# Scatters between zero columns in the Pool queue, and the fallback branch ahead of the last batch's scatters

## Chip, core, metric

The kernel runs on one core of a Trainium2 chip. The metric is the device time of one execution in microseconds (us), as a median over several executions. Ratios are the mean time of one kernel's fast runs over the mean of the other's fast runs of the same rounds, on the same chip, so they are not quite the ratio of the medians that stand beside them.

## The reference

```python
B, S, H = (8, 2048, 2560)          # scores (B, S, S), values (B, S, H), float32
best_j = np.argmax(scores, axis=2)
gathered = values[b_idx, best_j, :].copy()
out = np.zeros_like(values)
np.add.at(out, (b_idx, best_j, slice(None)), gathered)
```

Output row j of a batch is values row best_j of the position that chose it, summed over all positions whose argmax is j. Since the row added is always row j itself, the output row is `values[j]` times the number of times that j was chosen. So every row is of one of three kinds: never chosen (a zero row), chosen once (a plain copy), chosen more often (copy times a count).

## The kernel before

VectorE finds the argmax of each row of scores, TensorE counts with one-hot matrices, and the counts become three lists of row numbers for each batch. Pool then issues indirect DMAs of 128 rows each. Row numbers that are out of range are skipped, so a DMA may carry fewer than 128 rows.

- *copies* (`copy_once`): values to out inside the HBM, 16 a batch, for rows that were chosen once;
- *zero columns* (`zeros`): from a row of zeros in the SBUF, 7 a batch, 12 in the last one;
- *gather and scatter*: 5 each a batch. A gather brings 128 many-counted rows into one of six slots of `vbig`, ScalarE multiplies them by their counts, a scatter writes them out.

```python
        def gathers():
            for k in range(MCAP):                       # MCAP = 5
                v = stage()                             # next of 6 slots
                gather(v, mi[:, k:k + 1])
                nc.scalar.activation(out=v, in_=v, ..., scale=mc[:, k:k + 1])
                staged.append(v)
                if rest:
                    copy_once(rest.pop(0))

        def zeros():
            for k in range(ZLAST if b == B - 1 else ZCAP):     # 12 or 7
                scatter(zrow[:], zi[:, k:k + 1], free_running)
                if rest:
                    copy_once(rest.pop(0))
        ...
            gathers()
            zeros()
        for k in range(MCAP):
            scatter(staged[k], mi[:, k:k + 1])
        ...                                             # after all batches:
    nc.gpsimd.wait_ge(landed, 16 * n_free[0])
    more = nc.values_load(over_i[0:1, 0:1], engines=[mybir.EngineType.Pool], ...)
    with tc.If(more > 0):                               # lists longer than 7, 5 or 12 columns
        ...                                             # scatter and gather the rest
```

Copies and zero columns are `free_running`: they count on one semaphore, `landed`, that only the end waits for. Gathers and scatters have the framework's own semaphores ("tracked"). A gather must wait until the scatter that last read its slot has landed. In the last batch, `level_engines` (cut here) spreads the zero rows unevenly over 16 groups of partitions, so that all DMA engines get the same number of rows in total. The fallback in the `If` isn't taken for this draw. When a branch isn't taken, the framework's code for that path waits for all tracked DMAs issued before it, and then adds to their semaphores what the branch would have added; that is the `INC_SWDGE_SEM` of the profiles.

Of the kernel before, what the change touches and what calls it, by code (L numbers as in the profile page):

```python
# [36 lines left out]
def kernel(  # L37
# [6 lines left out]
    nc = tc.nc  # L44
    B, S, S2 = scores.shape
    _, _, H = values.shape
    assert S == S2
    NT = S // P
# [6 lines left out]
    NM = NT // 2  # L55
    NE = 16
    LE = P // NE
    ZCAP, MCAP = 7, 5
    ZLAST = 12
    CORR = 56  # L60

    values_flat = values.rearrange("b s h -> (b s) h")
# [56 lines left out]
    zrow = ctx.enter_context(nc.sbuf_tensor([P, H], FP32))  # L119
# [6 lines left out]
    zero_i = ctx.enter_context(nc.sbuf_tensor([P, B * NT], INT32))  # L126
    many_i = lists.tile([P, B * NM], INT32)
# [7 lines left out]
    landed = tc.alloc_semaphore("landed")  # L135
    n_free = [0]
# [8 lines left out]
    def gather(v, idx):  # L145
        nc.gpsimd.indirect_dma_start(  # L146
            out=v, out_offset=None, in_=values_flat[:, :],
            in_offset=bass.IndirectOffsetOnAxis(ap=idx, axis=0), bounds_check=B * S - 1, oob_is_err=False)

    def scatter(v, idx, note=writes_out):  # L150
        note(nc.gpsimd.indirect_dma_start(  # L151
            out=out_flat[:, :], out_offset=bass.IndirectOffsetOnAxis(ap=idx, axis=0),
            in_=v, in_offset=None, bounds_check=B * S - 1, oob_is_err=False))

    vslot = [0]

    def stage():
        v = vbig[:, vslot[0] * H:(vslot[0] + 1) * H]
        vslot[0] = (vslot[0] + 1) % NV
        return v  # L160
# [46 lines left out]
    def level_engines(rank):  # L207
# [27 lines left out]
        fits = lev.tile([P, 1], FP32)  # L235
        nc.vector.tensor_single_scalar(out=fits[:], in_=zeros, scalar=float(NE * (NT * LE - CORR)), op=ALU.is_le)
        nc.vector.tensor_scalar(out=more[:], in0=more[:], scalar1=float(CORR), scalar2=fits[:, 0:1], op0=ALU.min, op1=ALU.mult)
        all_more = lev.tile([P, 1], FP32)
# [29 lines left out]
    def value_steps(b, cnt_ps):  # L268
# [12 lines left out]
        def copy_once(t):  # L281
            free_running(scatter_rows_in_dram(
                nc, out_flat[:, :], values[b, t * P:(t + 1) * P, :], one_i[:, t:t + 1], last_row))
# [68 lines left out]
        rest = list(range(first, NT))  # L352
        staged = []

        def gathers():
            for k in range(MCAP):
                v = stage()
                gather(v, mi[:, k:k + 1])
                nc.scalar.activation(out=v, in_=v, func=mybir.ActivationFunctionType.Copy, bias=0.0,  # L359
                                     scale=mc[:, k:k + 1])  # L360
                staged.append(v)
                if rest:
                    copy_once(rest.pop(0))

        def zeros():
            for k in range(ZLAST if b == B - 1 else ZCAP):
                scatter(zrow[:], zi[:, k:k + 1], free_running)
                if rest:
                    copy_once(rest.pop(0))


        if b == 0:
            zeros()

            for _ in range(10):
                yield
            gathers()
        else:
            gathers()
            zeros()  # L380
        for k in range(MCAP):
            scatter(staged[k], mi[:, k:k + 1])
        yield

    ET = mybir.EngineType
    with tc.manual_schedule(engines={ET.PE, ET.DVE, ET.Activation, ET.SP}):
        pending = iter(())
        for b in range(B):
            cnt_ps = psum_c.tile([P, NT], FP32)
            for _ in count_steps(b, cnt_ps):  # L390
                next(pending, None)
            for _ in pending:
                pass
            pending = value_steps(b, cnt_ps)
            if b < 2:
                for _ in range(4):
                    next(pending)
        for _ in pending:
            pass
        full = fin.tile([1, 2], FP32)  # L400
        nc.vector.tensor_reduce(out=full[:, 0:1], in_=tots[0:1, 0, 0:B - 1], op=ALU.max, axis=mybir.AxisListType.X)
        nc.vector.tensor_reduce(out=full[:, 1:2], in_=tots[0:1, 1, :], op=ALU.max, axis=mybir.AxisListType.X)
        over = fin.tile([1, 3], FP32)
        nc.vector.tensor_single_scalar(out=over[:, 0:1], in_=full[:, 0:1], scalar=float(ZCAP * P), op=ALU.is_gt)
        nc.vector.tensor_single_scalar(out=over[:, 1:2], in_=full[:, 1:2], scalar=float(MCAP * P), op=ALU.is_gt)
        nc.vector.tensor_single_scalar(out=over[:, 2:3], in_=most[0:1, :], scalar=float(ZLAST * LE), op=ALU.is_gt)
        over_i = fin.tile([1, 1], INT32)
        nc.vector.tensor_reduce(out=over_i[:], in_=over[:], op=ALU.max, axis=mybir.AxisListType.X)

    nc.gpsimd.wait_ge(landed, 16 * n_free[0])  # L410
    more = nc.values_load(over_i[0:1, 0:1], engines=[mybir.EngineType.Pool], min_val=0, max_val=2)
    with tc.If(more > 0):
        for b in range(B):
            for k in range(ZLAST if b == B - 1 else ZCAP, NT):
                scatter(zrow[:], zero_i[:, b * NT + k:b * NT + k + 1])
            for k in range(MCAP, NM):
                v = stage()
                i = b * NM + k
                gather(v, many_i[:, i:i + 1])
                nc.gpsimd.tensor_scalar(out=v, in0=v, scalar1=many_c[:, i:i + 1], scalar2=None, op0=ALU.mult)  # L420
                scatter(v, many_i[:, i:i + 1])


# [28 lines left out]
```

## Time and profile before

| | before |
|---|---|
| time, median of 6 runs | 840.62 us (839.85 to 841.81) |
| profiled span | 838.4 us |
| last row landed (the trace's semaphore updates) | 829.95 us |
| from there to the end of the span, "tail" | 8.4 us |
| VectorE's last instruction ends | 697.2 us |

What bounds the kernel is read in the prediction below. Four stretches more of the kernel before will be needed later (us from and to, length; busy time of PE and PEld, which are TensorE, DVE, which is VectorE, ACT, which is ScalarE, and POOL; granted clock; mean busy share of the 16 DMA engines; GB/s):

```profile
635.00:640.00 5.00, 0.00 (x0) 0.00 (x0) 4.97 (x4) 0.00 (x0) 3.35 (x5) 1.00 0.99 389
695.00:700.00 5.00, 0.59 (x16) 0.48 (x15) 1.42 (x12) 0.00 (x0) 1.51 (x2) 1.00 0.93 385
790.00:795.00 5.00, 0.00 (x0) 0.00 (x0) 0.00 (x0) 3.76 (x2) 3.78 (x5) 1.00 1.01 424
795.00:800.00 5.00, 0.00 (x0) 0.00 (x0) 0.00 (x0) 2.43 (x1) 3.83 (x4) 1.00 1.01 424
```

The DMA moves about 424 GB/s where all 16 engines have work. At 635 and 695 us it is lower; I read this as some engines having nothing queued.

### The profile page before, as it was taken

To read this page: it belongs to the slowest core of one execution; us is meant where nothing else is said; L and a number is where in the kernel's file an instruction comes from. 1 tells how busy PE (TensorE), PEld (TensorE's weight loads), DVE (VectorE), ACT (ScalarE), POOL (GpSimd) and SP (SyncE) were. 2 spreads that over 40 slices of the span, in tenths; PEclk is the share of its full clock that TensorE was granted. 3 is DMA by queue.
4 is the path that set the end of the run, shared out by engine and by line. 5 is a ranking of instruction groups with operands and counts; after the bars stand their busy time and mean duration, and the time that the engine had idled before them with its cause. 6 is when DMAs were issued, how large, how long until landed. Compare 5 with 4: busy or idle time off the path is not lost.

```text
span 838.4 us, 2053 instructions
## 1 busy us (share of the span) xinstructions
PE 14.7 (2%) x273; PEld 14.1 (2%) x273; DVE 678.6 (81%) x794; ACT 102.9 (12%) x43; POOL 274.3 (33%) x277
## 2 busy tenths in 40 slices
PE   0000000000000000000000000000000000000000
PEld 0000000000000000000000000000000000000000
DVE  7999999999999999999999999999999992000000
ACT  2000001401300002200003200013100500500500
POOL 0000743267101254130263300551305724734720
DMA  9999999999999999999999999999999999999992
GB/s 383 426 429 431 380 421 422 421 407 428 422 431 426 425 427 431 426 426 427 427 428 428 428 427 425 429 425 427 427 426 409 420 425 412 417 416 418 418 418 117
DMA packets 48111, 347.04 MB, mean 414 GB/s; under 512 B 19014, under 2 KB 19014, under 8 KB 19014
## 3 DMA queue, kind: packets, MB, share of 16 engines
q0 software_dynamic: 38736, 212.67, 61.4%
q1 hardware_dynamic: 9360, 134.22, 37.6%
q14 instruction: 13, 0.11, 0.0%
q8 instruction: 2, 0.03, 0.0%
HBM read 354.42 MB, written 300.15 MB: 781 GB/s over the span
## 4 chain that ended last, share of the span: by engine, by line
DVE 69%; DMA 12%; POOL 5%; issue 4%; another core or an unknown queue 4%; ACT 0%; PE 0%; POOLq 0%
DVE am L185 32%; DVE mx L184 29%; DMA out_dram<-vbig,many_i 9%; DMA vbig<-in_values_dram,many_i 3%; POOL out_dram L151 2%; DVE oh_lo L194 2%; POOL out_dram L33 2%; DVE oh L321 2%; POOL vbig L146 1%; DVE lo L190 1%; DMA vbig<-in_scores_dram 1%; DVE oh_hi L198 0%; ACT vbig L359 0%; DVE put L336 0%
## 5 line engine op out<-in xcount | busy, mean ns | idle before, releaser
L185 DVE FIND_INDEX8 am<-mx,s_tile 128x8 uint32<-128x2048 f32 x116 | 265.0, 2285 | 0.0
L184 DVE MAX8 mx<-s_tile 128x8 f32<-128x2048 f32 x116 | 264.3, 2278 | 0.0
L33 POOL DMA_INDIRECT out_dram<-in_values_dram,ones_i x128 | 131.2, 1025 | 157.1 <-DVE m L292 119.0
L359 ACT ACTIVATE vbig<-vbig,many_c 128x2560 f32<-128x2560 f32 x40 | 96.7, 2426 | 693.8 <-DMA vbig<-in_values_dram,many_i 693.8
L146 POOL DMA_INDIRECT vbig<-in_values_dram,many_i x40 | 42.4, 1060 | 230.2 <-DMA out_dram<-vbig,many_i 182.3
L151 POOL DMA_INDIRECT out_dram<-vbig,many_i x40 | 38.9, 972 | 122.5 <-ACT vbig L359 118.0
L151 POOL DMA_INDIRECT out_dram<-zrow,zero_i x61 | 60.6, 994 | 18.9 <-issue 18.9
L184 DVE MAX8 mx<-vbig 128x8 f32<-128x2048 f32 x12 | 27.4, 2279 | 4.8 <-DMA vbig<-in_scores_dram 4.8
L185 DVE FIND_INDEX8 am<-mx,vbig 128x8 uint32<-128x2048 f32 x12 | 27.4, 2285 | 0.0
L194 DVE TENSOR_TENSOR oh_lo<-lo,lane_f 128x512 bf16<-128x512 uint32 x32 | 22.2, 693 | 0.4
L321 DVE TENSOR_TENSOR oh<-lo,fill_f 128x2048 f16<-128x2048 uint32 x8 | 18.3, 2291 | 0.3
L203 PE MATMUL cnt_ps<-oh_hi,oh_lo 128*128 128x16 bf16 x128 | 8.1, 174 | 578.3 <-DVE oh_hi L198 578.3
L203 PEld LDWEIGHTS <-oh_lo 128*128 128x128 bf16 x128 | 8.4, 105 | 578.1 <-DVE oh_lo L194 577.1
L185 DVE MATCH_VALUE_LOAD am<-mx,s_tile 128x8 f32 x116 | 10.7, 92 | 4.0
L198 DVE TENSOR_TENSOR oh_hi<-hi,lane_f 128x64 bf16<-128x64 uint32 x32 | 6.9, 217 | 0.0
L190 DVE TENSOR_SCALAR lo<-am 128x4 uint32<-128x4 uint32 x32 | 5.8, 183 | 1.1
L339 PE MATMUL l_ps<-put,oh 128*128 128x32 f16 x128 | 4.7, 188 | 68.5 <-DVE put L336 68.5
L339 PEld LDWEIGHTS <-oh 128*128 128x128 f16 x128 | 4.6, 104 | 69.6 <-DVE oh L321 59.2
L192 DVE TENSOR_SCALAR hi<-am 128x4 uint32<-128x4 uint32 x32 | 5.5, 172 | 0.0
L326 DVE TENSOR_TENSOR ez<-hi,lane_f 128x256 f16<-128x256 uint32 x8 | 3.3, 418 | 0.0
L336 DVE TENSOR_TENSOR put<-ez,row_f 128x256 f16<-128x256 f16 x8 | 3.3, 417 | 0.0
L347 DVE TENSOR_SCALAR e<-l_ps 128x32 f32<-128x32 f32 x8 | 1.5, 185 | 2.0 <-PE l_ps L339 2.0
(91 smaller groups left out, 60.3 us busy)
## 6 DMA issues: line engine op xcount, KB each, us to landing
s_tile<-in_scores_dram SPq DMA_DIRECT2D x58, 2048.0 KB, 12.0
vbig<-in_scores_dram SPq DMA_DIRECT2D x5, 2048.0 KB, 32.6
vbig<-in_scores_dram SPq DMA_DIRECT2D x2, 1024.0 KB, 6.1
out_dram<-in_values_dram,ones_i POOLq DMA_INDIRECT x128, 28.3
out_dram<-zrow,zero_i POOLq DMA_INDIRECT x61, 25.4
vbig<-in_values_dram,many_i POOLq DMA_INDIRECT x40, 32.3
out_dram<-vbig,many_i POOLq DMA_INDIRECT x40, 46.4
```

The source lines that it names most:

```text
L33: return eng.add_instruction(ins)
L146: nc.gpsimd.indirect_dma_start(out=v, out_offset=None, in_=values_flat[:, :], in_offset=bass.IndirectOffsetOnAxis(ap=idx, axis=0), bounds_ ...
L151: note(nc.gpsimd.indirect_dma_start(out=out_flat[:, :], out_offset=bass.IndirectOffsetOnAxis(ap=idx, axis=0), in_=v, in_offset=None, bound ...
L184: nc.vector.max(out=mx[:], in_=rows)
L185: nc.vector.max_index(out=am[:, g, :], in_max=mx[:], in_values=rows)
L190: nc.vector.tensor_single_scalar(out=lo[:], in_=am[:, :, 0], scalar=P - 1, op=ALU.bitwise_and)
L194: nc.vector.tensor_tensor(out=oh_lo[:], in0=lo[:].unsqueeze(2).to_broadcast([P, G, P]), in1=lane_f[:].unsqueeze(1).to_broadcast([P, G, P]) ...
L198: nc.vector.tensor_tensor(out=oh_hi[:], in0=hi[:].unsqueeze(2).to_broadcast([P, G, NT]), in1=lane_f[:, 0:NT].unsqueeze(1).to_broadcast([P, ...
L203: nc.tensor.matmul(out=cnt_ps[:], lhsT=oh_lo[:, g, :], rhs=oh_hi[:, g, :], start=(t == 0), stop=(t == NT - 1))
L321: nc.vector.tensor_tensor(out=oh[:], in0=lo[:].unsqueeze(2).to_broadcast([P, NT, P]), in1=fill_f[:].unsqueeze(1).to_broadcast([P, NT, P]), ...
L339: nc.tensor.matmul(out=l_ps[:], lhsT=oh[:, t, :], rhs=put[:, t, :], start=(t == 0), stop=(t == NT - 1))
L359: nc.scalar.activation(out=v, in_=v, func=mybir.ActivationFunctionType.Copy, bias=0.0, scale=mc[:, k:k + 1])
```

## The change

Its intent: scatters go ahead of the last three zero columns of a batch, so that slots come free sooner and Pool has work queued behind them. In the last batch the branch goes ahead of the scatters and of 8 zero columns, so that its cost lies under moving data and not at the end. The fallback uses one slot instead of cycling through six. (Cut: the declarations of `ZHEAD`, `last_staged` and `nz`, which is 12 in the last batch and 7 in the others, batch 0, where all zero columns stay ahead of the gathers, and the fallback's body, where only `v = stage()` moves out of the loops.)

```diff
-        def zeros():
-            for k in range(ZLAST if b == B - 1 else ZCAP):
+        def zeros(columns):
+            for k in columns:
...
         else:
             gathers()
-            zeros()
+            zeros(range(ZHEAD))                    # ZHEAD = 4
+        if b == B - 1:
+            while rest:
+                copy_once(rest.pop(0))
+            last_staged.extend(staged)
+            return
         for k in range(MCAP):
             scatter(staged[k], mi[:, k:k + 1])
+        if b > 0:
+            zeros(range(ZHEAD, nz))
...
-    nc.gpsimd.wait_ge(landed, 16 * n_free[0])
     more = nc.values_load(over_i[0:1, 0:1], engines=[mybir.EngineType.Pool], min_val=0, max_val=2)
     with tc.If(more > 0):
...
+    b = B - 1
+    for k in range(MCAP):
+        scatter(last_staged[k], many_i[:, b * NM + k:b * NM + k + 1])
+    for k in range(ZHEAD, ZLAST):
+        scatter(zrow[:], zero_i[:, b * NT + k:b * NT + k + 1], free_running)
+    nc.gpsimd.wait_ge(landed, 16 * n_free[0])
```

More of the change, by code (lines that the diff above doesn't have):

```diff
@@ L59 @@
     ZLAST = 12
+    ZHEAD = 4
     CORR = 56
@@ L155 @@
     vslot = [0]
+    last_staged = []
     def stage():
@@ L369, in zeros @@
                     copy_once(rest.pop(0))
+        nz = ZLAST if b == B - 1 else ZCAP
         if b == 0:
-            zeros()
+            zeros(range(nz))
             for _ in range(10):
@@ L379, in value_steps @@
             gathers()
-            zeros()
+            zeros(range(ZHEAD))
[4 more added lines that the diff above has]
+            return
         for k in range(MCAP):
             scatter(staged[k], mi[:, k:k + 1])
+        if b > 0:
+            zeros(range(ZHEAD, nz))
+        assert not rest
         yield
@@ L408 @@
         nc.vector.tensor_reduce(out=over_i[:], in_=over[:], op=ALU.max, axis=mybir.AxisListType.X)
-    nc.gpsimd.wait_ge(landed, 16 * n_free[0])
     more = nc.values_load(over_i[0:1, 0:1], engines=[mybir.EngineType.Pool], min_val=0, max_val=2)
     with tc.If(more > 0):
+        v = stage()
         for b in range(B):
@@ L416 @@
             for k in range(MCAP, NM):
-                v = stage()
                 i = b * NM + k
```

## The prediction

> **What bounds the kernel now.** I read the page first (parts 1, 2, 3), then the table of stretches, the waits of Pool, the time line of Pool at the end, and last the lines of the end of the program one by one.
>
> ```profile
> PE 14.7 (2%) x273; PEld 14.1 (2%) x273; DVE 678.6 (81%) x794; ACT 102.9 (12%) x43; POOL 274.3 (33%) x277
> ```
>
> The first line is a trap: VectorE is 81% busy, but the time line ends its last reduction at 697.2 us, and the span is 838.4. What is busy to the end is the DMA.
>
> ```profile
> DMA  9999999999999999999999999999999999999992
> q0 software_dynamic: 38736, 212.67, 61.4%
> q1 hardware_dynamic: 9360, 134.22, 37.6%
> ```
>
> Queue q1 (the scores) and q0 (all that Pool issues) together fill 99% of 16 engines' span. 212.67 MB of rows is exactly 20,762 rows of 10,240 bytes: 16,384 rows of the output, plus 4,378 rows that are counted twice or more and are moved twice (gather, then scatter). I counted those from the reference's own draw. The change moves no byte fewer. The stretches of the end (us; then busy time of PE, PEld, DVE, ACT, POOL; clock; DMA share; GB/s):
>
> ```profile
> 740.00:760.00 20.00, 0.00 (x0) 0.00 (x0) 0.00 (x0) 0.00 (x0) 2.04 (x2) 1.00 1.02 419
> 780.00:800.00 20.00, 0.00 (x0) 0.00 (x0) 0.00 (x0) 12.14 (x5) 15.18 (x16) 1.00 1.02 425
> 820.00:825.00 5.00, 0.00 (x0) 0.00 (x0) 0.00 (x0) 0.00 (x0) 0.00 (x0) 1.00 0.54 227
> 825.00:830.00 5.00, 0.00 (x0) 0.00 (x0) 0.00 (x0) 0.00 (x0) 0.00 (x0) 1.00 0.17 72
> 830.00:835.00 5.00, 0.00 (x0) 0.00 (x0) 0.00 (x0) 0.00 (x0) 0.00 (x0) 1.00 0.00 0
> ```
>
> Pool does nearly nothing from 740 to 760 and still the DMA share is 1.02. So Pool's long waits,
>
> ```profile
> POOL vbig L146 <- DMA out_dram<-vbig,many_i: 182.3, 19, 41.5
> POOL out_dram L151 <- ACT vbig L359: 118.0, 25, 9.9
> ```
>
> (gathers that wait for a slot of vbig, scatters that wait for the multiplication) lie over a full queue and cost almost nothing. Two things are left at the end: a fall of the DMA share from 820 to 830, where some of the 16 engines are done and others are not, and 8.4 us after the last landing (830.0) in which nothing moves. That tail is made of these:
>
> ```profile
> L410 POOLq EVENT_SEMAPHORE  x1: 17/17/17, 817.2 to 817.2; - x1
> L411 POOLq TENSOR_LOAD <-over_i x1: 626/626/626, 817.3 to 817.3; - x1
> L412 POOLq COMPARE_BRANCH  x1: 53/53/53, 818.2 to 818.2; - x1
> L412 POOLq EVENT_SEMAPHORE  x5: 17/43/43, 822.2 to 830.0; - x5
> L412 POOLq INC_SWDGE_SEM  x1: 1340/1340/1340, 830.1 to 830.1; - x1
> L447 POOLq DRAIN  x3: 40/107/6121, 831.4 to 838.1; - x3
> ```
>
> At 817.2 the rows that carry no tile semaphore have landed; the register load and the branch follow; the path where the branch is not taken begins at 822.2 and waits on the semaphores of gathers and scatters until 830.0; one instruction that adds to those semaphores takes 1.34 us; a Pool drain takes 6.12 us; barriers take 0.8 us.
>
> **What the Trainium skill says.** "DMA: Bandwidth & Descriptors", Issuing engines are not separate DMA queues: DMAs of all issuers run on the same 16 engines and interleave. The trace agrees (share 1.02 with q0 alone, 1.01 with both), so a new order in Pool's queue creates no bandwidth. The same page, Why a DMA increments its semaphore by 16 and not by 1: each engine posts its own +1, and only the full 16 means landed. The trace agrees and shows how much that matters here: the 16 updates of the last gather stand from 777.6 to 795.1 us, so the engines run up to 17.5 us apart. "Runtime: NRT & Kernel Launch", Instruction fetch mechanics: a taken branch out of the fetched window stalls for a fetch. The trace agrees: 3.9 us from the end of the branch (818.3) to the next instruction (822.2). No page states what a Pool drain behind software DMAs costs.
>
> **The change part by part.** *(a) Batches 1 to 6: five scatters go ahead of zero columns 4 to 6 and the three copies between them.* Same instructions. They land earlier by what now stands behind them: about 258 zero rows (770 less 4 x 128) and 3 x 45 copied rows, 393 rows or 25 to an engine. An engine moves 418/16 = 26.1 GB/s, a row in 0.39 us: 10 us. So Pool's wait for slots should shrink by some 8 to 10 us a batch, but that wait is covered by the DMA. What it can recover is the time in which leading engines ran dry. In 5-us stretches from 620 to 815 the rate fell visibly below 425 at 630 to 640 (407, 382), 695 to 705 (394, 404) and a few more; all deficits there sum to about 3.4 us of the mean engine, and a part of that is skipped rows, not idleness. I put down 0 to 3 us.
>
> *(b) Last batch: the branch ahead of the scatters.* The register load (0.63), the arithmetic (0.19) and the branch with its fetch (4.0) were already hidden in the fall from 817 to 830; they gain nothing. The add to the semaphores (1.34) leaves the tail. The drain (6.12) stands at the end of the program in both kernels. If it is a walk over everything Pool has issued, it stays; if it is work left over by the add, it goes. The price: the untaken path waits, as now, for every tracked DMA issued before it, and the last of them is now the fifth gather of the last batch. It landed at 795.1 on the slowest engine. Until then Pool issues none of the 5 scatters and 8 zero columns behind it.
>
> Does the DMA run dry meanwhile? I replayed the levelling code on the draw. All engines get 1,298 or 1,299 rows (one 1,293), but the zeros of the last batch per engine are between 20 and 76: the engines that had many copied rows lag, the others lead and get more zeros. Behind the fifth gather stand 8 copies and zero columns 0 to 3. *Slowest engine*: 24 + 20 = 44 rows, 17 us, busy until 812: the scatters come long before. *Leading engine* (76 zeros): 777.6 us, then 21 copied rows and 32 zeros, 53 x 0.39 = 21 us: dry at 798. The first scatter can start at 795.1 + 0.1 + 1.34 + 1.0 (one indirect DMA on Pool, 0.97 in its row of part 5) + about 1 of start = 798.5. So it is just caught. Behind it: 34 scattered rows and 44 zeros, 78 x 0.39 = 30 us, then about 1 us to land: 829.5. Before, it was 777.6 + 131 rows = 828 to 830. *The last landing hardly moves.* Pool's 13 issues at 1.28 us end at about 814 and are not the limit.
>
> *(c) Fallback branch with a single slot*: not taken for this draw (7 x 128 = 896 against at most 780 zeros; 5 x 128 = 640 against 565; 12 x 8 = 96 against 76). No time.
>
> Sum: last landing 829.5 (was 830.0), no add, drain 6.1 and barriers 0.9: span 836.5. The median stands 2.3 us above the profiled span, so about 838.7; with (a)'s gain at the slowest engine, up to 2 us less.
>
> **The rivals.** *The drain is a leftover of the add.* It starts 0.03 us after the add ends, and by then Pool had issued nothing for 28 us, which speaks for it; that the drain at the program's start took 0.2 us with no DMA behind it speaks for the other reading. If the leftover also blocks nothing behind it, the tail falls to about 1 us: 832.5. If it blocks Pool's next issue instead, the first scatter comes at 804.5, the leading engines idle 6 us, the landing goes to 835.5 and the tail to 1 us: 838.5, again no gain. I give the drain 70% to stay.
>
> *The slots free earlier and the engines close up.* The mean engine was done at about 822.4 (the 16 updates of the last scatter stand from 815.7 to 830.0), so perfect levelling would gain 7 us more, with the drain kept 831, without it 825. Against it: the chain above ties the leading engines to the slowest engine's fifth gather, which is not moved by freeing slots, since all work ahead of it in the ring is the same.
>
> *The branch becomes a real wait.* Under a full DMA the fetch of the untaken path may take longer than 4 us, and the leading engines may be further ahead, as (a) lets them run: each us by which the first scatter comes later than they run dry is a us on the end. With 4 to 6 us lost: 843.
>
> **Range and chances.** 70% for the drain kept (836 to 840), about 20% for the drain gone (829 to 834), the rest for a lengthened landing. Weighted I say 837.0, range 830.0 to 843.0. Faster by over 2% means below 824.1: it would need the drain gone and the engines levelled at once, 5%. Slower by over 2% means above 857.4, 17 us lost: 3%.
>
> **What would show it.** In the profile after: bytes and packets of q0 unchanged; the DMA share 1.0 until about 820; Pool's wait for slots clearly below 182 us, with the total hardly moved; the first scatter of the last batch issued 2 to 3 us after the fifth gather's full landing near 795; the last landing at 829.5 +/- 3; a drain of about 6 us at the end and no add ahead of it. It is wrong if the drain is under 1 us (then I mis-assigned it), if the first scatter comes 8 us after the gather (the add blocks), or if the fall of the DMA share at the end becomes much shorter than 15 us (then levelling, which I discounted, was the gain).

## The result

The changed kernel takes 839.79 us (median of 6 runs, 838.97 to 840.14) against 840.62; the ratio is 0.9989 with an interval of 0.9976 to 1.0002. That can't be told from no change. The profiled span is 837.9 us. It is inside the range, but the forecast of 837.0 was a gain of 3.6 us, and 0.8 came.

The same stretches of the changed kernel, with those of the end:

```profile
635.00:640.00 5.00, 0.00 (x0) 0.00 (x0) 4.93 (x6) 0.00 (x0) 3.78 (x5) 1.00 1.02 422
695.00:700.00 5.00, 0.59 (x16) 0.58 (x16) 3.73 (x16) 0.00 (x0) 4.32 (x3) 1.00 1.02 422
790.00:795.00 5.00, 0.00 (x0) 0.00 (x0) 0.00 (x0) 3.66 (x3) 0.00 (x0) 1.00 0.96 400
795.00:800.00 5.00, 0.00 (x0) 0.00 (x0) 0.00 (x0) 1.29 (x1) 2.81 (x3) 1.00 0.84 350
...
820.00:825.00 5.00, 0.00 (x0) 0.00 (x0) 0.00 (x0) 0.00 (x0) 0.00 (x0) 1.00 0.47 172
825.00:830.00 5.00, 0.00 (x0) 0.00 (x0) 0.00 (x0) 0.00 (x0) 0.00 (x0) 1.00 0.09 37
```

The low stretches at 635 and 695 us are filled. A new and deeper one stands between 790 and 800, where there was none before. Pool's waits (us in total, times, longest):

```profile
POOL out_dram L152 <- ACT vbig L361: 237.4, 35, 25.3
...
POOL vbig L147 <- DMA out_dram<-vbig,many_i: 80.5, 16, 18.1
```

The wait for slots fell from 182.3 to 80.5 us, and the wait for the multiplication rose from 118.0 to 237.4. Most of both lies over a full DMA queue. The last one does not. It shows in Pool's time line:

```profile
776.98 0.98 POOL L33 DMA_INDIRECT out_dram<-in_values_dram,ones_i  x1 [0.30 <-issue]
796.58 0.97 POOL L152 DMA_INDIRECT out_dram<-vbig,many_i  x1 [18.62 <-ACT vbig L361]
```

Pool issues nothing for 18.6 us. The view puts that down to the multiplication; the instructions of the branch, and the last line of the end of the program, say what it was:

```profile
L422 POOLq EVENT_SEMAPHORE  x5: 17/43/14687, 772.7 to 793.9; - x5
L422 POOLq COMPARE_BRANCH  x1: 53/53/53, 767.6 to 767.6; - x1
L422 POOLq INC_SWDGE_SEM  x1: 1381/1381/1381, 794.0 to 794.0; - x1
...
L464 POOLq DRAIN  x3: 40/107/7675, 829.4 to 837.6; - x3
```

The path that isn't taken waits 14.7 us, until the fifth gather has landed on the slowest DMA engine at 793.8, and adds to the semaphores for 1.38 us; 2.8 us after that landing the first scatter goes out. The last row lands at 829.20 us, 0.75 earlier than before, which is less than this moment varies from profile to profile (see below). The add is gone from the tail. But the Pool drain at the end takes 7.68 us instead of 6.12, so the tail is 8.7 us and not the 7.0 that I had summed.

Two questions are left. Why did the filled stretches bring only 0.75 us? And why did the drain grow?

### The profile page after: what moved, and what is told of

Its sections match the earlier page's. It is cut to its first block, busy times and chain, and to the rows that moved or that the text cites. A ratio compares the mean times of both kernels' runs of the same rounds, so it can differ in the third digit from the quotient of the medians.

```text
span 837.9 us, 2055 instructions
## 1 busy us (share of the span) xinstructions
PE 14.7 (2%) x273; PEld 14.2 (2%) x273; DVE 679.8 (81%) x794; ACT 103.0 (12%) x43; POOL 273.5 (33%) x277
## 3 DMA queue, kind: packets, MB, share of 16 engines
q0 software_dynamic: 38736, 212.67, 61.3%
## 4 chain that ended last, share of the span: by engine, by line
DVE 70%; DMA 13%; issue 6%; POOL 5%; another core or an unknown queue 2%; PE 0%; POOLq 0%
DVE am L187 32%; DVE mx L186 30%; DMA out_dram<-vbig,many_i 8%; DMA vbig<-in_values_dram,many_i 5%; DVE oh_lo L196 2%; POOL out_dram L152 2%; POOL out_dram L33 2%; DVE oh L323 2%; POOL vbig L147 1%; DVE lo L192 1%; DMA vbig<-in_scores_dram 1%; DVE oh_hi L200 0%; DVE hi L194 0%; DVE put L338 0%
## 5 line engine op out<-in xcount | busy, mean ns | idle before, releaser
L152 POOL DMA_INDIRECT out_dram<-vbig,many_i x40 | 39.7, 992 | 238.9 <-ACT vbig L361 237.4
L147 POOL DMA_INDIRECT vbig<-in_values_dram,many_i x40 | 41.3, 1032 | 128.0 <-DMA out_dram<-vbig,many_i 80.5
```

What stands on the lines that cost most here:

```text
L147: nc.gpsimd.indirect_dma_start(out=v, out_offset=None, in_=values_flat[:, :], in_offset=bass.IndirectOffsetOnAxis(ap=idx, axis=0), bounds_ ...
L152: note(nc.gpsimd.indirect_dma_start(out=out_flat[:, :], out_offset=bass.IndirectOffsetOnAxis(ap=idx, axis=0), in_=v, in_offset=None, bound ...
```

## The experiments

My theory after the result: part (a), the order in batches 1 to 6, lets the leading DMA engines run on without a gap, which is worth several us at the end; part (b), the branch, makes the same engines wait for the slowest one and takes it back. The rival: neither matters for the last landing, since it is fixed by the bytes of the slowest engine. On the drain: it is a walk over the DMAs that Pool has issued and not yet struck off; or it has a fixed cost; or it is left over from the add.

| kernel | last landing | tail | span | median | ratio to before (95% interval) |
|---|---|---|---|---|---|
| before | 829.95 | 8.42 | 838.37 | 840.62 | |
| changed | 829.20 | 8.70 | 837.90 | 839.79 | 0.9989 (0.9976 to 1.0002) |
| a_only | 824.81 | 10.22 | 835.03 | 836.86 | 0.9968 (0.9955 to 0.9982) |
| b_only | 830.09 | 7.14 | 837.23 | 839.01 | 0.9989 (0.9976 to 1.0003) |
| no_branch | 825.83 | 8.64 | 834.47 | 836.26 | 0.9964 (0.9951 to 0.9978) |
| pinned_drain | 828.18 | 4.94 | 833.12 | 835.66 | 0.9954 (0.9940 to 0.9968) |
| zeros_first | 824.91 | 4.68 | 829.59 | 831.38 | 0.9903 (0.9888 to 0.9918) |
| zeros_first_drain | 824.76 | 4.94 | 829.70 | 831.45 | 0.9905 (0.9889 to 0.9920) |
| old_order_zeros_first | 830.01 | 3.90 | 833.91 | 835.72 | 0.9947 (0.9933 to 0.9960) |

The last landing is the last update of a DMA semaphore in the trace; the tail is the span less that. The kernel before was run beside each group; its median there was 840.08, 839.55 and 839.96 us. All outputs were correct. Each last landing is that of one profile. Four profiles in which the rows go out in the same order (changed, early_drain, drain_in_between, pinned_drain) have it between 828.2 and 829.2 us, so a difference of 1 us in this column tells nothing.

### a_only

The edit, against the changed kernel: the last batch and the branch as in the kernel before.

```diff
-            zeros(range(ZHEAD))
-        if b == B - 1:
-            while rest: ...
-            return
+            zeros(range(nz if b == B - 1 else ZHEAD))
         ...
-        if b > 0:
+        if 0 < b < B - 1:
             zeros(range(ZHEAD, nz))
```

> Part (a) alone: batches 1 to 6 in the new order, the last batch and the branch as in the kernel before. Theory (the end is set by engines that ran dry earlier): the low stretches at 630-640 and 695-705 us fill up to about 422 GB/s, nothing runs dry at 790-800 either, as no branch gates the scatters; the last landing comes at 825 to 828 (830.0 before), the tail stays 8.4 us with a drain near 6.1, ratio to before 0.995 to 0.998. Rival (slots that come free earlier are worth nothing, the last landing is fixed by the bytes of the slowest engine): last landing 829.5 to 830.5, ratio 0.999 to 1.001.

```profile
635.00:640.00 5.00, 0.00 (x0) 0.00 (x0) 4.96 (x4) 0.00 (x0) 3.85 (x4) 1.00 1.03 424
...
795.00:800.00 5.00, 0.00 (x0) 0.00 (x0) 0.00 (x0) 1.32 (x1) 0.96 (x1) 1.00 1.02 426
...
825.00:830.00 5.00, 0.00 (x0) 0.00 (x0) 0.00 (x0) 0.00 (x0) 0.00 (x0) 1.00 0.00 0
```

No stretch is as low as before (first two lines; at 695 us it is 414 GB/s), and nothing is in flight after 825: the last landing comes at 824.8, 5.1 us earlier than before. The rival falls: freeing slots does move the end. It moves it by letting the engines end closer together: in both kernels the last DMA is a scatter, and its 16 updates, one for each engine, stand from 815.7 to 830.0 us with a mean of 823.5 before, and from 814.9 to 824.8 with a mean of 821.6 here. But the tail grew to 10.2 us. The end of the program shows it:

```profile
L418 POOLq INC_SWDGE_SEM  x1: 1592/1592/1592, 824.9 to 824.9; - x1
L453 POOLq DRAIN  x3: 40/107/7672, 826.5 to 834.8; - x3
```

I had expected a drain of 6.1 us; it is 7.67, with the branch where it had always been. So the new order lengthens the drain, not the branch.

### b_only

The edit, against the changed kernel: `zeros(range(nz))` ahead of the scatters in batches 1 to 6, as before; the last batch as changed.

> Part (b) alone: old order in batches 1 to 6, the branch ahead of the last batch's scatters. Theory (the branch makes the leading engines wait for the slowest engine's fifth gather): the low stretches of before stay at 630-640, and one more appears between 790 and 800, smaller than the 403 and 348 GB/s of the changed kernel because the leading engines are less far ahead; last landing 829 to 831, add gone from the tail, ratio 0.998 to 1.001. Rival (the gate costs nothing): last landing 826 to 828 and ratio below 0.996.

```profile
635.00:640.00 5.00, 0.00 (x0) 0.00 (x0) 4.97 (x4) 0.00 (x0) 3.58 (x4) 1.00 0.98 389
...
795.00:800.00 5.00, 0.00 (x0) 0.00 (x0) 0.00 (x0) 2.32 (x1) 2.03 (x3) 1.00 1.02 422
L462 POOLq DRAIN  x3: 40/107/6123, 830.3 to 837.0; - x3
```

The last landing (830.1) and the ratio are as my theory had them, but the low stretch between 790 and 800 that it expected isn't there: 422 GB/s. My reading: with the old order the leading engines (those whose queues run ahead of the others') have lost their lead at 635 and 695 us and have none left to lose at the branch, so they wait in one place or in the other. The fifth gather's first update agrees: it comes at 777.6 us here, as before, and at 771.4 in the changed kernel. The drain is at 6.12 us again, so its length goes with the order in batches 1 to 6: 6.12 in both kernels with the old order, 7.66 to 7.68 in the three with the new one and nothing else done to it.

### no_branch

The edit, against the changed kernel: register load, branch and fallback removed, which is right for this draw only.

> The changed kernel without the register load, the branch and the fallback (right for this draw, which doesn't take it). Theory (the gate costs what part (a) gained): the first scatter of the last batch is issued near 782, when its own gather is through, not at 796.6; no low stretch at 790-800; last landing 825 to 827 (829.2 with the branch), ratio to before 0.993 to 0.996. Rival (the gate is harmless, the end is set elsewhere): last landing 828.5 to 829.5, ratio 0.998 to 1.0. On the drain: if it is a walk over what Pool has issued it takes 6 to 8 us here too; if it were left over from the add to the semaphores, which is not in this kernel, it takes under 1 us.

```profile
781.94 0.97 POOL L152 DMA_INDIRECT out_dram<-vbig,many_i  x1 [4.01 <-ACT vbig L361]
...
L452 POOLq DRAIN  x3: 45/101/7662, 826.0 to 834.2; - x3
```

The first scatter goes out at 781.9 instead of 796.6, and the 795 to 800 us stretch is at 424 GB/s. The last landing is 825.8, so the branch costs the changed kernel 3.4 us there (829.2 less 825.8). The ratio, 0.9964, lies just beyond the theory's range. The drain is 7.66 us without any add: it isn't left over from the add.

### early_drain and drain_in_between

Both put one more Pool drain into the changed kernel, `nc.gpsimd.drain()`, and both told nothing: the scheduler saw no reason to keep it in its place and moved it to the start of the program (0.91 us there in both). Their times, 839.51 (5 rounds; ratio 0.9995, 0.9981 to 1.0008) and 839.65 us (one look, state unknown), are those of the changed kernel. The expectations:

> The changed kernel with one Pool drain more, ahead of the wait for the last rows, right after Pool's last issue (near 813). If the 7.7 us of the final drain are a walk over finished entries, that walk now lies under the rows still in flight: the added drain ends within 1 us of the last landing (near 829), the final drain takes under 0.5 us, span 830 to 831, ratio to before 0.989 to 0.992. If a Pool drain after DMAs costs a fixed 6 to 8 us once all is landed, the added one ends near 836 and the time doesn't fall: ratio 0.998 to 1.001.

> A measurement of the drain, slower on purpose: the changed kernel with a Pool drain between the branch and the last 13 DMAs. That drain must wait for all rows in flight (near 812), so the last DMAs start some 16 us late and the time rises by 10 to 20 us. Walk theory: the final drain has only 13 entries left to go over and takes under 2 us instead of 7.7. Rival (fixed cost of a drain after DMAs): the final drain still takes 6 to 8 us.

### pinned_drain

The edit, against the changed kernel, with the order of Pool's instructions fixed by hand:

```diff
+    with tc.manual_schedule(engines={ET.Pool}):
         for k in range(MCAP):
             scatter(last_staged[k], ...)
         for k in range(ZHEAD, ZLAST):
             scatter(zrow[:], ..., free_running)
+        nc.gpsimd.drain()
         nc.gpsimd.wait_ge(landed, 16 * n_free[0])
```

> The changed kernel with one more Pool drain, this time pinned behind Pool's last issue (in the earlier try the scheduler had moved it to the program's start, so that run told nothing). Walk theory (a Pool drain goes over the finished DMAs that Pool has not yet struck off, at a cost for each): the added drain starts near 812 and ends within 1 us of the last landing (near 829), the program's final drain takes under 0.5 us, span 830 to 831.5, ratio to before 0.989 to 0.993. Rival (a drain costs a fixed 6 to 8 us once all has landed): the added drain ends near 836, ratio 0.998 to 1.001 or above.

The added drain, and the program's own one:

```profile
L439 POOLq DRAIN  x1: 29948/29948/29948, 802.1 to 802.1; - x1
L466 POOLq DRAIN  x3: 34/43/107, 832.3 to 832.9; - x3
```

The added one lasts until 832.0, 3.85 us after the last landing, and the program's own drain then takes 0.04 us. So the drain's cost here is not a fixed one, and what it does can lie under moving rows, but not all of it: 3.85 us are left, just half of 7.67. The expected ratio of 0.989 to 0.993 was missed (0.9954), since the added drain ended 3.85 us after the last landing and not within 1 us of it.

### drain_after_first

The same, with the drain behind the first of the last 13 DMAs; one look, state unknown, slower on purpose (852.5 us).

> The drain measured again, since in the run before the scheduler had once more moved the added drain to the start: here it is pinned behind the first of the last 13 DMAs of the changed kernel, so the final drain has only 12 DMAs left to go over. It is slower on purpose (12 DMAs start some 20 us late). Walk theory: from 1.34 to 1.59 us for the add and 6.12 to 7.67 us for the drain between the two orders I estimate some 0.1 us for a DMA in the drain, so the final drain takes 0.8 to 1.6 us. Rival (a cost for any drain that has something to strike off): 6 to 8 us.

```profile
L467 POOLq DRAIN  x3: 46/107/1041, 848.9 to 850.5; - x3
```

The final drain has 12 DMAs to go over and takes 1.04 us, 0.087 us for each. So its length goes with what has been issued since the last drain: it is a walk over DMAs not yet struck off, or over their descriptors, which these runs don't tell apart. By that figure (an estimate from this run), 7.67 us are some 88 DMAs and 6.12 us some 70, of the 269 that both kernels issue. The add, which no run was made for, agrees: it took 1.13, 1.22, 1.34, 1.38, 1.48 and 1.59 us in b_only, old_order_zeros_first, before, changed, zeros_first and a_only, and by the estimate, less the DMAs issued behind the add, 57, 65, 70, 75, 83 and 88 were then not struck off. Why the new order leaves 18 more, no run shows.

### zeros_first

Against the changed kernel, all 12 zero columns of the last batch stand ahead of the branch, with only the 5 scatters behind it.

```diff
-            zeros(range(ZHEAD))
+            zeros(range(nz if b == B - 1 else ZHEAD))
 ...
-    for k in range(ZHEAD, ZLAST):
-        scatter(zrow[:], zero_i[...], free_running)
```

> The changed kernel with all 12 zero columns of the last batch ahead of the branch, only the 5 scatters behind it. Gate theory: the leading engines now have their zeros while Pool waits for the fifth gather, so nothing runs dry at 790-800 (above 418 GB/s); last landing 824 to 826 as in the run of part (a) alone, no add in the tail, drain 7.7: span 833 to 834.5, ratio 0.993 to 0.996. Rival (the gate's cost is the wait of Pool itself): last landing 828 to 830, ratio 0.998 or above.

```profile
795.00:800.00 5.00, 0.00 (x0) 0.00 (x0) 0.00 (x0) 1.41 (x1) 2.60 (x3) 1.00 1.02 426
...
L462 POOLq DRAIN  x3: 40/107/15944, 812.8 to 829.3; - x3
```

Pool waits at the branch as long as before (14.7 us), but now the leading engines have their zeros queued behind the fifth gather and don't run dry: 426 GB/s. The last landing is 824.9, as in a_only. The span beat my expectation by 3.4 us and more, for a reason that I hadn't seen: the wait for `landed` ends at 812.6 now, since the last rows are scatters, which that semaphore doesn't count. So the program's own drain starts at 812.8, under the last scatters, and ends 3.85 us after the last landing. Of the 8.3 us between the spans of the changed kernel and this one, 4.3 are the earlier last landing and 4.0 the shorter tail. **This kernel beats both**: 831.38 us, ratio 0.9903.

### zeros_first_drain

zeros_first with the pinned drain behind its last scatter.

> Both of the former: zero columns ahead of the branch and the pinned drain behind the last scatter. If both theories hold the gains add: last landing 824 to 826, tail of about 1 to 1.5 us, span 825.5 to 827.5, ratio to before 0.983 to 0.987. If the walk doesn't overlap: ratio 0.993 to 0.996.

The ratio, 0.9905, is that of zeros_first, so both expected ranges were missed. The program's own drain was early enough; starting one at 798.4 instead of 812.8 changes nothing, it still ends 3.86 us after the last landing.

### old_order_zeros_first

zeros_first with the old order in batches 1 to 6.

> The faster version (zero columns of the last batch ahead of the branch, scatters behind it) but with the old order in batches 1 to 6: what part (a) is worth inside it. If (a) is worth what it gave alone (last landing 824.8 against 830.0), the last landing is 829.5 to 830.5 here, the low stretches at 630-640 and 695-705 are back, span 833.5 to 835.5 and ratio to before 0.993 to 0.996 (the faster version 0.990). Rival (the gain of the faster version is all in its last batch): ratio 0.990 here too.

```profile
635.00:640.00 5.00, 0.00 (x0) 0.00 (x0) 4.97 (x4) 0.00 (x0) 3.67 (x4) 1.00 0.97 377
...
L460 POOLq DRAIN  x3: 40/107/15621, 817.5 to 833.6; - x3
```

The low stretch is back, the last landing is 830.0 and the ratio 0.9947. So inside the faster version part (a) moves the last landing by 5.1 us again, as it did alone; 0.8 us of that go to the longer drain. This drain ends 3.1 us after the last landing, half of 6.12.

## Why the prediction was right or wrong

**What bounds the kernel: right.** The bytes of q0 (212.67 MB) and its packets (38,736) are unchanged, the DMA is full from 620 to 815 us but for the stretches named, and Pool's waits moved by more than 100 us each with 0.75 us at the end to show for it. But that the waits "cost almost nothing" was wrong for the slots: a_only shortens the wait for them and lands 5.1 us earlier, which the branch hid in the changed kernel.

**The gate in part (b): right, with one size off.** I had derived the last landing from the slowest engine's fifth gather (795.1) through add, issue and 78 rows to 829.5; the gather landed at 793.8, the first scatter followed 2.8 us later, and the last landing was 829.2. I had the leading engines "just caught" at 798. They ran dry before: the updates of the fifth gather that the trace has begin at 771.4 instead of 777.6 us, as part (a) had let them run ahead; with my 21 us of queued rows (an estimate) they were dry at about 792, and the DMA share fell to 0.84. The third rival had named this. Its 843 us didn't come: the first scatter was no later than I had reckoned, and with it the end of those engines; what they lost was the lead that (a) had given them.

**Part (a): mechanism right, size wrong.** I had put down 0 to 3 us, read as the mean over 16 engines. Alone it moves the mean engine by 2.0 us (823.5 to 821.6), as I had it, but the last landing by 5.1 (a_only), and the end is set by the last engine. The changed kernel shows little of it: 4.4 us are gone again between a_only and the changed kernel (824.8 to 829.2), 3.4 of them at the branch (no_branch); the other 1.0 is no more than profiles of one order differ by. Two readings of mine were off: the view has 408, 389, 385 and 408 GB/s where I wrote 407, 382, 394 and 404, and the mean of the 16 updates is 823.5 and not 822.4.

**The step that failed: "The drain (6.12) stands at the end of the program in both kernels."** It stands there, but it didn't stay 6.12: it measured 7.68, and the 1.55 us more ate the 1.34 us of the add that left the tail. In the first rival I gave the drain about 20% to go altogether, and this, with part (a)'s "up to 2 us less", pulled my point from the sum's 838.7 to 837.0. pinned_drain and drain_after_first show what it goes with: 0.087 us for each DMA that Pool has not struck off. Why there were more of them stays open. With the term at 7.68 the sum would have been about 840.3.

**The levelling rival**: I discounted it with the chain through the fifth gather. That was right for the changed kernel and only for it. Without the branch ahead of the scatters (a_only), or with the zero columns ahead of the branch (zeros_first), the chain is cut, and the gain is there.

**What stays open.** Why the new order leaves more DMAs to walk over, and why half of the walk is left after the last landing in these runs (3.85 of 7.67, 3.86 of 7.67, 3.1 of 6.12). The added drain of drain_after_first fits too: it ended at 818.2, 3.4 us after the last landing ahead of it (814.9), where 76 DMAs would be 6.6 us by the estimate.

## What to carry to other kernels

When engines run apart and any of them can set the end, ask of each moved wait which engine will run dry behind it: time won at one wait can be lost at the next, and two changes that are each reasonable can cancel. Put work that needs nothing ahead of a gate and not behind it; here this turned no gain into 1%, about half of it because the gap behind the gate was filled, and half because the end's drain could begin earlier. In this kernel the end of the program had a cost that grew with the indirect DMAs of Pool not yet struck off, and half of it was hidden where rows were still moving when it began: look for such a drain at the end of yours.

## What the Trainium skill lacked or had wrong

- "VectorE: DVE Perf Modes", The DRAIN you can't avoid, calls the runtime's drains at a program's start and end about 12 ns, constant, on all 5 engines. Pool's first drain at the end took 6.12 us in the kernel before and 7.68 us in the changed one; SyncE's took 7 ns. The trace puts them down to the kernel's own line 447 (464), so they may not be of the kind that the page means; then what it lacks is this kind.
- No page has what a Pool drain costs behind indirect DMAs: 0.087 us for each DMA not yet struck off (1.04 us for 12, one run), 0.04 us where another drain has just ended, and half of the walk left after the last landing in the runs where it began earlier.
- No page has the cost of the semaphore add on the path that isn't taken: 1.13 to 1.59 us in these runs, behind a wait for every tracked DMA ahead of it (14.7 us here).
- "Runtime: NRT & Kernel Launch", Instruction fetch mechanics, gives the stall of a branch out of the fetched window without a time. From the branch to the next instruction it was 3.9 us in the kernel before, with the DMA share falling from 0.91 to 0.54, and 5.0 us in the changed one, with the DMA full. In both a packet of the instruction queue starts within that gap (820.7 and 771.1 us).
